# Two small sums and minima of a softmax written as reductions over two neighbouring columns

## The chip, the cores and the metric

The kernel runs on one core of a Trainium2 chip. The metric is device time of one execution in microseconds (us); lower is better. The engines named below work beside each other, each through its own queue in order: TensorE (PE, with its weight loads as PEld), VectorE (DVE), ScalarE (ACT), GpSimd (POOL) and SyncE (SP, which here issues transfers). SBUF is the on-chip working memory, PSUM the memory that TensorE writes to.

## What is computed

The program is one step of a two-layer trunk over 256 context tokens and 1024 latent tokens of width 1024, in float32. The change lies in the first layer's grouped-query attention of the latent tokens (8 query heads, 2 key heads, 1024 latent keys and 256 cached context keys in one softmax):

```
keys = jnp.concatenate([axial_rope(k), ctx_k.astype(k.dtype)], axis=1)
values = jnp.concatenate([vals, ctx_v.astype(vals.dtype)], axis=1)
b_out = blocked_attention(axial_rope(q), keys, values)
...
def one_block(qblk):
    s = jnp.einsum('bqngd,bsnd->bngqs', qblk, k).astype(jnp.float32) * scale
    p = jax.nn.softmax(s, axis=-1).astype(v.dtype)
    return jnp.einsum('bngqs,bsnd->bqngd', p, v)
```

The softmax needs one maximum and one denominator for each row of 1280 scores.

## The kernel before

The whole program is written for one core with the order of every engine's instructions fixed by hand: in the attention, each job has a table of events at fractional slots, and `run_jobs` emits the events of up to four jobs that overlap, sorted by slot. So a row of an engine's queue is where the table puts it, and an engine does its queue in that order.

In the latent attention a job is one pair of 128-query tiles (a = 0 and 1) of one head; there are 32 such jobs (4 pairs of tiles, 8 heads), then two jobs of another class for the context tokens. The 1280 scores of a tile come in two parts: 1024 latent scores in a PSUM tile of class A (`scores`, L704 and L705) and 256 cached ones in PSUM tile C (`cached_scores`, L711 and L712). For each part there is a negated maximum (`maxima`, L719 and L717) and, from the exponential's accumulator, a part of the denominator (`exp`, L730). So each tile has two maxima in neighbouring columns of a small SBUF tile `sm` and two partial denominators in two other neighbouring columns. `bias` (L723) takes the smaller of the two negated maxima. `scale` adds the two denominators (L734), takes the reciprocal (L735), and then lets POOL multiply the 1280 probabilities by it in two instructions of 640 columns (L737). All of `bias`, L734 and L735 are DVE instructions on 128 x 1 elements.

After that the scaled probabilities are transposed by TensorE into a PSUM tile B (`turn`, L374, four 128 x 128 blocks at a time), split into a high part by ACT (`hi`, L384) and a low part by DVE (`lo`, L390), and multiplied with the values (`values`, L408). `store` (L355 on ACT, L356 on DVE) ends a job. In every eighth job the queries of the next pair of tiles are also loaded and split, by ACT (L637) and POOL (L638); such a job is called a query-loading job below.

In one period of the steady stage, DVE's order is: lo 4 of an older job, lo 0, maxima 0, lo 1, the cached maxima, store, bias 0, lo 2, scale 1, lo 3, maxima 1, scale 0, bias 1. So of a job's two L734, that of tile 0 stands ahead of a bias and two L390, and that of tile 1 between two L390.

Of the kernel before, what the change touches and what calls it, by code (L numbers as in the profile page):

```python
# [15 lines left out]
ALU = mybir.AluOpType  # L16
AX = mybir.AxisListType
# [32 lines left out]
def trunk_kernel(ctx: ExitStack, tc: tile.TileContext, A: dict, O: dict):  # L50
    nc = tc.nc
    PE, ACT, DVE, POOL, SP = nc.tensor, nc.scalar, nc.vector, nc.gpsimd, nc.sync
# [147 lines left out]
    def rstd_of(ss, n, scale, eps=EPS):  # L200

        v, r = sm(n), sm(n)
        DVE.tensor_scalar(v, ss, scale, eps, op0=ALU.mult, op1=ALU.add)
        POOL.tensor_tensor(r, v, mhalf[:, 0:n], op=ALU.pow)  # L204
        return r
# [444 lines left out]
    def gate_steps(l, w):  # L650

        for j in range(2):
            c = slice(512 * j, 512 * j + 512)
            total = [t2([P, 512]) for _ in range(2)]
            for k in range(KT):
                r = raw([P, 512])
                SP.dma_start(r, A["mod_w"][l, rows(k), (3 * w + 2) * D + 512 * j : (3 * w + 2) * D + 512 * j + 512])
                yield
                for c in range(2):
                    if k == 0:  # L660
                        DVE.tensor_scalar(total[c], r, cond[:, k, c : c + 1], None, op0=ALU.mult)
                    else:
                        DVE.scalar_tensor_tensor(total[c], r, cond[:, k, c : c + 1], total[c], op0=ALU.mult, op1=ALU.add)
            bias, acc = raw([32, 512]), bank((32, 512))
            SP.dma_start(bias, A["mod_b"][l, 3 * w + 2, 32 * j : 32 * j + 32])
            for c in range(2):
                PE.matmul(acc, pick[:, c, :], total[c], start=c == 0, stop=c == 1)
            yield
            DVE.tensor_tensor(bias, acc, bias, op=ALU.add)
            SP.dma_start(gate_d[l, w, :, 512 * j : 512 * j + 512], bias[0:2])  # L670
# [16 lines left out]
    class Latent(Job):  # L687
# [32 lines left out]

        def bias(self, a):
            m = self.sm[:, 2 * a : 2 * a + 2]
            DVE.tensor_tensor(self.sm[:, 8 + a : 9 + a], m[:, 0:1], m[:, 1:2], op=ALU.min)  # L723

        def exp(self, a, c):
            if self.p[a] is None:
# [4 lines left out]

        def scale(self, a):
            z, p = self.sm[:, 10 + a : 11 + a], self.p[a]
            DVE.tensor_tensor(z, self.sm[:, 4 + 2 * a : 5 + 2 * a], self.sm[:, 5 + 2 * a : 6 + 2 * a], op=ALU.add)  # L734
            DVE.reciprocal(z, z)  # L735
            for c in (slice(0, 640), slice(640, 1280)):
                POOL.tensor_tensor(p[:, c], p[:, c], z.to_broadcast([P, 640]), op=ALU.mult)  # L737
# [967 lines left out]
```

## Time and profile before

| what | value |
|---|---|
| median of 3 runs | 3441.93 us (3436.46 to 3443.43) |
| the profiled execution | 3447.16 us |
| its span, first to last instruction | 3445.4 us |
| granted TensorE clock, mean | 0.982 of full speed |
| busy: PE | 3265.6 us (95%) |
| busy: DVE | 2094.1 us (61%) |
| busy: ACT | 1266.3 us (37%) |
| busy: POOL | 1179.4 us (34%) |

The busy times are sums over the whole span; the latent attention is only its part from about 205 to 466 us. All durations quoted further on come from the profiled execution, which lies 5.2 us (0.15%) above the median of the runs and has 1.8 us outside its span.

### The profile page before, as it was taken

To read this page: it belongs to the slowest core of one execution; us is meant where nothing else is said; L and a number is where in the kernel's file an instruction comes from. 1 tells how busy PE (TensorE), PEld (TensorE's weight loads), DVE (VectorE), ACT (ScalarE), POOL (GpSimd) and SP (SyncE) were. 2 spreads that over 40 slices of the span, in tenths; PEclk is the share of its full clock that TensorE was granted. 3 is DMA by queue.
4 is the path that set the end of the run, shared out by engine and by line. 5 is a ranking of instruction groups with operands and counts; after the bars stand their busy time and mean duration, and the time that the engine had idled before them with its cause. 6 is when DMAs were issued, how large, how long until landed. Compare 5 with 4: busy or idle time off the path is not lost. (4 is left out here: it accounts for less than half of the span.)

```text
span 3445.4 us, 44445 instructions
## 1 busy us (share of the span) xinstructions
PE 3265.6 (95%) x17258; PEld 2723.2 (79%) x17258; DVE 2094.1 (61%) x3589; ACT 1266.3 (37%) x2529; POOL 1179.4 (34%) x742
## 2 busy tenths in 40 slices
PE   5789999999999999999899999999999999999998
PEld 3667777888878878888778888887778888888886
DVE  7879988546666664344866666666574444344347
ACT  3467863451111111112566666656531111111113
POOL 3556667451111111113644433335221111111134
PEclk8889999999999999999999999999999999999999
DMA  5210023442222221112411111113431111111124
GB/s 208 69 37 14 19 89 114 155 145 87 87 87 88 88 84 40 38 37 86 177 58 45 47 47 45 49 65 97 126 116 45 39 42 43 37 37 37 38 91 165
DMA packets 106211, 260.03 MB, mean 75 GB/s; under 512 B 10240, under 2 KB 45952, under 8 KB 106000
## 3 DMA queue, kind: packets, MB, share of 16 engines
q1 hardware_dynamic: 106000, 257.20, 22.5%
q8 instruction: 135, 2.21, 0.3%
q14 instruction: 76, 0.62, 0.1%
HBM read 221.34 MB, written 35.82 MB: 75 GB/s over the span
## 5 line engine op out<-in xcount | busy, mean ns | idle before, releaser
L1097 DVE TENSOR_TENSOR s<-s,B 128x512 f32<-128x512 f32 x840 | 559.9, 685 | 565.2 <-PE B L192 564.5
L176 POOL TENSOR_TENSOR w<-raw,w 128x1024 fp32r<-128x1024 f32 x163 | 402.6, 2472 | 1408.0 <-ACT w L175 1403.8
L190 PE MATMUL A<-hh,w 128*128 128x512 f32 (+1 forms) x2112 | 755.0, 357 | 3.5 <-DVE s L330 2.2
L192 PE MATMUL A<-hh,w 128*128 128x512 f32 (+1 forms) x2112 | 750.3, 355 | 2.8 <-POOL w L176 2.8
L191 PE MATMUL A<-hl,w 128*128 128x512 f32 (+1 forms) x2112 | 747.7, 354 | 0.0
L190 PEld LDWEIGHTS A<-hh,w 128*128 128x128 f32 x2112 | 397.5, 188 | 69.5 <-issue 5.9
L192 PEld LDWEIGHTS A<-hh,w 128*128 128x128 f32 x2112 | 397.2, 188 | 66.0 <-POOL w L176 4.0
L191 PEld LDWEIGHTS A<-hl,w 128*128 128x128 f32 x2112 | 397.4, 188 | 62.8
L175 ACT CAST w<-raw 128x1024 fp32r<-128x1024 f32 x166 | 174.2, 1049 | 712.7 <-PE B L191 416.1
L190 PE MATMUL B<-w,s 128*128 128x512 f32 x880 | 351.2, 399 | 14.2 <-DVE s L1097 13.5
L192 PE MATMUL B<-w,s 128*128 128x512 f32 x880 | 348.2, 396 | 9.7 <-DVE s L176 8.7
L191 PE MATMUL B<-w,s 128*128 128x512 f32 x880 | 344.0, 391 | 0.0
L1078 ACT ACTIVATE t<-A,c 128x512 f32<-128x512 f32 (+1 forms) x132 | 81.2, 615 | 703.2 <-PE A L192 703.2
L374 PE MATMUL B<-c,s 128*128 128x128 f32 x1344 | 205.8, 279 | 46.8 <-DVE w L390 23.4
L374 PEld LDWEIGHTS B<-c,s 128*128 128x128 f32 x1344 | 155.8, 141 | 90.6 <-DVE w L390 35.7
L190 PE MATMUL C<-hh,w 128*128 128x512 f32 (+1 forms) x576 | 213.0, 370 | 5.2 <-ACT s L1200 1.8
L390 DVE TENSOR_TENSOR t<-B,t 128x512 fp32r<-128x512 f32 (+2 forms) x216 | 127.6, 591 | 142.9 <-ACT t L384 129.6
L190 PEld LDWEIGHTS B<-w,s 128*128 128x128 f32 x880 | 165.3, 188 | 59.2 <-DVE s L1097 27.0
L1079 DVE TENSOR_TENSOR t<-t,A 128x512 f32<-128x512 f32 (+1 forms) x132 | 78.9, 598 | 218.6 <-ACT t L1078 218.6
L192 PEld LDWEIGHTS B<-w,s 128*128 128x128 f32 x880 | 165.4, 188 | 52.5 <-DVE s L176 12.7
L192 PE MATMUL C<-hh,w 128*128 128x512 f32 (+1 forms) x576 | 205.4, 357 | 0.0
L191 PE MATMUL C<-hl,w 128*128 128x512 f32 (+1 forms) x576 | 205.3, 356 | 0.0
(283 smaller groups left out, 6178.9 us busy)
## 6 DMA issues: line engine op xcount, KB each, us to landing
raw<-wall SPq DMA_DIRECT2D x171, 512.0 KB, 3.3
raw<-mod_w SPq DMA_DIRECT2D x72, 512.0 KB, 3.9
x_d<-s SPq DMA_DIRECT2D x30, 512.0 KB, 2.6
w<-wall SPq DMA_DIRECT2D x22, 512.0 KB
raw<-x SPq DMA_DIRECT2D x20, 512.0 KB, 3.9
s<-x_d SPq DMA_DIRECT2D x20, 512.0 KB
s<-wall SPq DMA_DIRECT2D x17, 512.0 KB, 3.4
w<-mod_w SPq DMA_DIRECT2D x16, 512.0 KB, 9.3
```

Of the source, the lines that this page charges most:

```text
L175: ACT.copy(hi, src)
L176: (eng or DVE).tensor_tensor(lo, src, f32(hi), op=ALU.subtract)
L190: PE.matmul(out, sh, mh, start=i == 0, stop=False)
L191: PE.matmul(out, sh, ml, start=False, stop=False)
L192: PE.matmul(out, sl, mh, start=False, stop=i == n - 1)
L374: PE.transpose(tr[:, at : at + P], self.p[a][:, col : col + P], ident)
L390: DVE.tensor_tensor(tl[:, 0:n], tr[:, 0:n], f32(th[:, 0:n]), op=ALU.subtract)
L1078: ACT.activation(s, acc[:, 0, 0:n], AF.Silu, bias=zerob)
L1079: DVE.tensor_tensor(s, s, acc[:, 1, 0:n], op=ALU.mult)
L1097: DVE.tensor_tensor(yt, yt, part, op=ALU.add)
```

## The change

`bias` and the addition in `scale` each used an instruction with two one-column inputs, `tensor_tensor`. They now use `tensor_reduce` over one input of two neighbouring columns, with the same operation (minimum, addition) and the same one-column output.

```
@@ -720,7 +720,7 @@
         def bias(self, a):
             m = self.sm[:, 2 * a : 2 * a + 2]
-            DVE.tensor_tensor(self.sm[:, 8 + a : 9 + a], m[:, 0:1], m[:, 1:2], op=ALU.min)
+            DVE.tensor_reduce(self.sm[:, 8 + a : 9 + a], m, axis=AX.X, op=ALU.min)
@@ -731,7 +731,7 @@
         def scale(self, a):
             z, p = self.sm[:, 10 + a : 11 + a], self.p[a]
-            DVE.tensor_tensor(z, self.sm[:, 4 + 2 * a : 5 + 2 * a], self.sm[:, 5 + 2 * a : 6 + 2 * a], op=ALU.add)
+            DVE.tensor_reduce(z, self.sm[:, 4 + 2 * a : 6 + 2 * a], axis=AX.X, op=ALU.add)
             DVE.reciprocal(z, z)
             for c in (slice(0, 640), slice(640, 1280)):
                 POOL.tensor_tensor(p[:, c], p[:, c], z.to_broadcast([P, 640]), op=ALU.mult)
```

It concerns 128 DVE instructions: 64 of L723 and 64 of L734, two of each in every latent job. No instruction is added, removed or moved: every engine's queue has the same rows in the same order, and each of the 128 waits for the same engine as before.

## Rows read from the trace of the kernel before

**Rows 1.** Busy time of each engine in two stretches: the attention, what follows it.
```profile
core 0: us, PE busy (x) PEld busy (x) DVE busy (x) ACT busy (x) POOL busy (x), PEclk, DMA share, GB/s
...
215.00:466.00 251.00, 225.19 (x1559) 192.47 (x1558) 240.92 (x453) 199.63 (x437) 169.61 (x138) 0.99 0.07 22
...
483.00:560.00 77.00, 75.78 (x355) 59.69 (x354) 68.55 (x105) 32.50 (x55) 51.03 (x31) 1.00 0.34 108
```
**Rows 2.** Groups by line and form, 200 to 480 us: busy us, mean ns | idle before.
```profile
L734 DVE TENSOR_TENSOR sm<-sm 128x1 f32<-128x1 f32 x64 | 34.5, 538 | 1.3 <-ACT s L730 1.3
...
L723 DVE TENSOR_TENSOR sm<-sm 128x1 f32<-128x1 f32 x64 | 15.8, 247 | 0.5
```
**Rows 3.** One line's instructions: minimum, median and maximum duration in ns.
```profile
L734 DVE TENSOR_TENSOR sm<-sm x64: 142/152/1019, 209.5 to 470.4; 128x1 f32<-128x1 f32 x64
...
L723 DVE TENSOR_TENSOR sm<-sm x64: 137/142/1223, 207.4 to 465.5; 128x1 f32<-128x1 f32 x64
```
**Rows 4.** DVE in order of time, one ordinary job: start us, duration us, instruction.
```profile
329.58 0.15 DVE L734 TENSOR_TENSOR sm<-sm 128x1 f32<-128x1 f32 x1
329.77 0.17 DVE L735 RECIPROCAL sm<-sm 128x1 f32<-128x1 f32 x1
...
331.57 1.02 DVE L734 TENSOR_TENSOR sm<-sm 128x1 f32<-128x1 f32 x1
332.62 0.16 DVE L735 RECIPROCAL sm<-sm 128x1 f32<-128x1 f32 x1
...
332.76 1.28 DVE L390 TENSOR_TENSOR w<-B,w 128x512 fp32r<-128x512 f32 x2
```
**Rows 5.** POOL, ACT and PE in the same job, in order of time.
```profile
330.10 2.47 POOL L737 TENSOR_TENSOR s<-s,sm 128x640 f32<-128x640 f32 x2 [2.68 <-DVE sm L735]
...
331.25 0.71 PE L374 MATMUL B<-c,s 128*128 128x128 f32 x4
...
331.99 0.59 ACT L384 CAST w<-B 128x512 fp32r<-128x512 f32 x1 [0.53 <-PE B L374]
...
332.49 0.40 PE L705 MATMUL A<-s,w 128*128 128x512 f32 x1
333.50 0.66 PE L374 MATMUL B<-c,s 128*128 128x128 f32 x4 [0.61 <-DVE w L390]
```
**Rows 6.** A query-loading job in order of time: DVE, ACT, POOL.
```profile
295.23 0.68 DVE L723 TENSOR_TENSOR sm<-sm 128x1 f32<-128x1 f32 x1
...
298.68 1.07 ACT L384 CAST w<-B 128x512 fp32r<-128x512 f32 x2
...
298.82 0.60 DVE L734 TENSOR_TENSOR sm<-sm 128x1 f32<-128x1 f32 x1 [0.33 <-ACT s L730]
...
299.48 2.60 POOL L638 TENSOR_TENSOR w<-raw,w 64x512 fp32r<-64x512 f32 x2
...
299.53 1.22 DVE L723 TENSOR_TENSOR sm<-sm 128x1 f32<-128x1 f32 x1
300.68 1.27 DVE L390 TENSOR_TENSOR w<-B,w 128x512 fp32r<-128x512 f32 x2
```
**Rows 7.** POOL and DVE in an earlier stage, in order of time.
```profile
69.11 2.35 POOL L176 TENSOR_TENSOR s<-raw,s 128x256 fp32r<-128x256 f32 x4 [2.03 <-ACT s L175]
...
70.36 0.69 DVE L479 TENSOR_REDUCE sm<-s 128x8 f32<-128x512 f32 x1 [0.36 <-ACT s L478]
71.08 0.40 DVE L203 TENSOR_SCALAR sm<-sm 128x8 f32<-128x8 f32 x1
```
**Rows 8.** POOL and DVE in the second layer's attention, in order of time.
```profile
1782.24 2.62 POOL L1273 TENSOR_TENSOR w<-s,w 64x1024 fp32r<-64x1024 f32 x1
...
1782.55 0.15 DVE L1421 RECIPROCAL sm<-sm 128x1 f32<-128x1 f32 x1
```
**Rows 9.** One line's instructions for other reductions: minimum, median and maximum ns.
```profile
L479 DVE TENSOR_REDUCE sm<-t x10: 276/285/289, 62.4 to 188.8; 128x2 f32<-128x128 f32 x10
L479 DVE TENSOR_REDUCE sm<-s x8: 677/679/687, 70.4 to 172.7; 128x8 f32<-128x512 f32 x8
...
L1409 DVE TENSOR_REDUCE sm<-A x128: 406/414/425, 1762.1 to 2404.9; 128x1 f32<-128x256 f32 x128
```

More of the change, by code (lines that the diff above doesn't have):

```diff
@@ L722, in bias @@
             m = self.sm[:, 2 * a : 2 * a + 2]
-            DVE.tensor_tensor(self.sm[:, 8 + a : 9 + a], m[:, 0:1], m[:, 1:2], op=ALU.min)
+            DVE.tensor_reduce(self.sm[:, 8 + a : 9 + a], m, axis=AX.X, op=ALU.min)
         def exp(self, a, c):
@@ L733, in scale @@
             z, p = self.sm[:, 10 + a : 11 + a], self.p[a]
-            DVE.tensor_tensor(z, self.sm[:, 4 + 2 * a : 5 + 2 * a], self.sm[:, 5 + 2 * a : 6 + 2 * a], op=ALU.add)
+            DVE.tensor_reduce(z, self.sm[:, 4 + 2 * a : 6 + 2 * a], axis=AX.X, op=ALU.add)
             DVE.reciprocal(z, z)
```

## The prediction

> **What bounds the kernel now.** I read the whole-kernel busy shares first, and they mislead here: PE is busy 95% of the span and DVE 61%, so a change on DVE looks free. The change touches only the latent attention, so the view that counts is the table of busy time by stretch [rows 1]. In the 251.0 us from 215 to 466 us, DVE is busy 240.92 us (96%), PE 225.19 us (90%), ACT 199.63 us (80%) and POOL 169.61 us (68%). In this stretch DVE is the fullest engine, and PE has some 26 us of gaps. After it, from 483 to 560 us, PE is busy 75.78 of 77.0 us (98%).
>
> Next, the groups by line for this stretch [rows 2]. The two lines of the diff do the same kind of work, one addition or minimum of one column, and should cost the same. L723 has a mean of 247 ns, L734 of 538 ns. The spread says more [rows 3]: both have a median near 0.15 us (142 and 152 ns) but maxima of 1223 and 1019 ns. So some instances stand still. The time order shows where [rows 4, 5]: the L734 at 329.58 takes 0.15 us with POOL idle; the one at 331.57 takes 1.02 us and ends at 332.59. POOL's two L737 run from 330.10 to 332.57. The addition, whose two inputs both lie in SBUF, is held until POOL's instruction ends. In the query-loading job the same happens to L723: it starts at 299.53, just after POOL's L638 at 299.48 (two in 2.60 us, so the first ends near 300.78), and ends at 300.75 [rows 6].
>
> Held time in all: 34.5 − 64 × 0.152 = 24.8 us for L734 and 15.8 − 64 × 0.142 = 6.7 us for L723, together 31.5 us [rows 2, 3]. Reading all 128 in order of time, I count 27 L734 of 0.95 to 1.02 us, one in each ordinary job but the first, and in each of the 4 query-loading jobs one L734 near 0.60 and two L723 near 0.67 and 1.22 us. As a check: 27 × 0.86 + 4 × 0.45 = 25.0 us for L734.
>
> **The change, part by part.**
> First, is a reduction held as well? The trace has one instance with an SBUF input beside a running POOL instruction [rows 7]: POOL's four L176 fill 69.11 to 71.46, and L479, a reduction of 128x512 from SBUF, starts at 70.36 and takes 0.69 us, its unhindered 679 ns [rows 9]. Right after it a TENSOR_SCALAR of 128x8 at 71.08 takes 0.40 us, until 71.48, when POOL is done. So in one and the same stretch the reduction passes and another form is held. I take it that L723 and L734 are no longer held.
>
> Second, the reduction's own price. No row has two columns. The reductions give 285 ns for 128 columns and 679 ns for 512 [rows 9], so (679 − 285) / 384 = 1.03 ns a column and, from 285 − 126 × 1.03, an estimated 155 ns for two. Bounds: no cheaper than the 137 ns minimum of L723 [rows 3], since nothing this short is cheaper; no dearer than 285 ns, the smallest SBUF reduction. I take 155, the straight line's value: 3 ns more on L734 and 13 ns more on L723, 64 × 0.016 = 1.0 us in all. The upper bound would cost 64 × (0.133 + 0.143) = 17.7 us if all of it lay on the path, the lower bound gives back 1.3 us.
> The Trainium skill speaks against the change in "VectorE: DVE Perf Modes", section "Rules for kernel authors": `tensor_reduce` runs at the base rate, is "the slowest DVE op" and is to be avoided on a hot path. The rows above put 1.03 ns on each column and a start of some 0.15 us, so by them the rule costs nothing at two columns; by the rule taken as a general penalty, at the 285 ns bound, the gain summed below would be 25.1 + 1.0 − 17.7 = 8.4 us.
>
> Third, an ordinary job. Without the hold, L735 follows the L734 of 331.57 by 0.19 us (as 329.77 does 329.58) and the first L390 follows L735 by 0.14 us (332.62 to 332.76) [rows 4]: it starts at 331.90 instead of 332.76, 0.86 us earlier. The second L390 of the pair would start 0.60 us later (1.28 for both, 0.68 for one), at 332.50. But it needs ACT's L384 of 331.99, which ends at 332.58 [rows 5]. That one waits for TensorE's transposes of 331.25 to 331.96, half of which read what POOL has scaled by 330.10 + 1.24 = 331.34; this chain starts from the unhindered L734 at 329.58 and doesn't get shorter. So the second L390 starts at 332.60 instead of 332.76 + 0.60 = 333.36: 0.76 us earlier, not 0.86. DVE's queue is full from there to the next 329.58-like L734, so all that follows moves with it. For TensorE: its transposes at 333.50 waited for the first L390 [rows 5], 0.61 us after the end of L705 at 332.89. L390 now ends at 331.90 + 0.68 = 332.58, and TensorE, whose score matmuls follow each other by 0.23 us, is ready at 332.72: a gain of 0.78 us. Both give 0.76 to 0.78 us; I take 0.76. 27 × 0.76 = 20.5 us.
>
> Fourth, a query-loading job [rows 6]. The L723 held at 295.23 saves nothing: the next L734, at 298.82, waits for ACT's exponential, and ACT is full there. Behind it, L734 loses 0.45 us and L723 1.08 us. The first L390 would start at 298.82 + 0.19 + 0.14 = 299.15 (with the ordinary job's spacings), needs the first of ACT's two L384 (298.68 + 0.59 = 299.27), and the second L390 needs the other (299.75) and 0.60 us after the first: 299.89 instead of 301.28. That is 1.39 us; 4 × 1.39 = 5.6 us.
>
> Sum: 20.5 + 5.6 − 1.0 = 25.1 us, of 31.5 us held. What comes after the attention is TensorE's [rows 1], with transfers at a 0.34 share, so the gain is kept. The profiled execution becomes 3447.2 − 25.1 = 3422.1 us, the median of the runs, 5.2 us lower, 3441.9 − 25.1 = 3416.8 us.
>
> **The rivals.**
> *The hold moves one instruction on.* The reciprocal L735 follows L734 and never ran beside POOL in this stretch before. If it is held, L734 to L390 takes as long as now. Against it: a reciprocal of the same shape ran 0.15 us at 1782.55 inside a POOL instruction [rows 8]. The same end is reached if a two-column reduction is held after all; one row [rows 7], of another shape, speaks against it. What would be left is at most the L723 part, 4 × 1.08 = 4.3 us: 3438 to 3442 us. Chance 0.09.
> *The gain is cut by another wait.* With DVE earlier, the ring over POOL, TensorE and ACT closes the period, and I followed it only at one job's places; ACT, 80% busy, orders its exponentials between the L384. If half the gain is lost: 3425 to 3435 us. Chance 0.14.
> *More than forecast.* If the L723 of 295.23 counts too and the ring gives way to the full 0.86 us, the gain is the held 31.5 us and some of TensorE's gaps: 3407 to 3411 us. Chance 0.05.
> *Slower.* A reduction costs DVE more than the hold does. Its place is DVE's queue, four of them a job; it decides from 0.76 / 4 = 0.19 us extra each, a reduction of 0.34 us. The next row above that, a one-column result at 414 ns [rows 9], would cost 4 × 0.26 − 0.76 = 0.28 us a job, 32 × 0.28 = 9 us: 3451 us. That row has 256 columns out of PSUM, and the line through the others leaves no room for it. Chance 0.03.
>
> **How the numbers follow.** The forecast has 0.69, with its own range 3411 to 3423 us. With the larger gain, and the nearer half of the cut one, the range 3407 to 3428 us holds about 8 in 10. About 0.2% (7 us) is what a measurement of this kernel can tell from no change: faster 0.88 (forecast, cut, larger), same 0.09, slower 0.03.
>
> **What the profile after would show.** L723 and L734 as TENSOR_REDUCE with minimum, median and maximum all near 0.15 us; their sum 64 × 0.31 = 19.8 us instead of 50.3; L735 unchanged at 0.16 us although POOL now runs beside it; POOL's second pair of L737 joined to the first; TensorE's wait for L390 ahead of its transposes gone; ordinary jobs about 7.3 us apart. I am wrong if L735 or the reductions show a tail, if the period shrinks by less than 0.5 us, or if a later stage gives it back.

## The result and the profile after

The changed kernel takes 3416.76 us (median of 4 runs, 3413.36 to 3417.94) against 3440.4 us of the kernel before (4 runs): a ratio of 0.993, 95% interval 0.9913 to 0.9948. Run again later beside three of the experiments, it took 3421.2 us against 3446.6 us, 0.9919 (0.9904 to 0.9935). The forecast was 3416.8 us.

The first rows to compare are those of the two lines, as in [rows 3]; with them the reciprocal that follows and POOL's scaling. Columns: count, minimum/median/maximum ns, first and last start.

```profile
L723 DVE TENSOR_REDUCE sm<-sm x64: 134/136/157, 206.0 to 437.1; 128x1 f32<-128x2 f32 x64
...
L734 DVE TENSOR_REDUCE sm<-sm x64: 143/145/157, 208.1 to 441.9; 128x1 f32<-128x2 f32 x64
...
L735 DVE RECIPROCAL sm<-sm x64: 163/164/167, 208.3 to 442.1; 128x1 f32<-128x1 f32 x64
...
L737 POOL TENSOR_TENSOR s<-s,sm x128: 1248/1253/1258, 208.6 to 443.7; 128x640 f32<-128x640 f32 x128
```

The tails of 1223 and 1019 ns are gone. In the kernel before, 39 of the 128 instructions (31 L734, 8 L723) started while POOL ran an instruction, and every one of them ended 0.01 to 0.02 us after that instruction's end; the other 89 started with POOL idle and took at most 164 ns. Now 74 of the 128 start beside a running POOL instruction, and none takes more than 157 ns. POOL's instructions take what they took (a median of 1256 ns before), so nothing was handed to it, and the reciprocal, which now runs beside POOL, was not held.

The same place in an ordinary job, in order of time (start us, duration us), which answers to [rows 4, 5]: DVE first, then POOL, ACT and PE.

```profile
315.55 0.14 DVE L734 TENSOR_REDUCE sm<-sm 128x1 f32<-128x2 f32 x1
...
317.52 0.15 DVE L734 TENSOR_REDUCE sm<-sm 128x1 f32<-128x2 f32 x1
317.70 0.17 DVE L735 RECIPROCAL sm<-sm 128x1 f32<-128x1 f32 x1
317.78 0.14 DVE L723 TENSOR_REDUCE sm<-sm 128x1 f32<-128x2 f32 x1
317.83 1.43 DVE L390 TENSOR_TENSOR w<-B,w 128x512 fp32r<-128x512 f32 x2
```
```profile
316.06 4.89 POOL L737 TENSOR_TENSOR s<-s,sm 128x640 f32<-128x640 f32 x4 [2.28 <-PE B L374]
```
```profile
317.95 0.59 ACT L384 CAST w<-B 128x512 fp32r<-128x512 f32 x1 [0.52 <-PE B L374]
```
```profile
318.45 0.40 PE L705 MATMUL A<-s,w 128*128 128x512 f32 x1
318.69 0.60 PE L374 MATMUL B<-c,s 128*128 128x128 f32 x4
```

POOL now works from 316.06 to 320.95 without a break, and the three small DVE instructions L734, L735 and L723 pass it at full speed. The pair of L390 starts 0.31 us after L734 and not 1.19. It takes 1.43 us where it took 1.28: the second waits for ACT's L384, which ends at 318.54, as the forecast's third step said. TensorE's transposes follow its score matmuls at 0.24 us, without the 0.61 us wait of [rows 5].

The busy time of the stretch, the row that answers to the first of [rows 1]:

```profile
core 0: us, PE busy (x) PEld busy (x) DVE busy (x) ACT busy (x) POOL busy (x), PEclk, DMA share, GB/s
215.00:442.00 227.00, 223.23 (x1583) 194.64 (x1580) 213.64 (x455) 198.48 (x443) 169.22 (x138) 1.00 0.09 28
```

PE is now busy 98% of the stretch and DVE 94%, where it was 90% and 96%. From the first maximum (L719) to the start of the last L734 the attention takes 441.93 − 203.90 = 238.03 us against 470.36 − 205.31 = 265.05 us: 27.0 us less. After it the program takes 2973.0 us against 2975.0 us: the gain is kept.

Not all of the 27.0 us belongs to the change. In the opening jobs TensorE's granted clock rises from 0.50 (the 1.2 GHz level) to 1.00 (2.4 GHz). In the kernel before it rises 12.6 us after the first maximum. In this profile of the changed kernel it rises 8.6 us after it, in the second profile of the same kernel (the change once more, below) 12.7 us after it. The rows show 4 us of each, from 8 to 12 us after the first maximum: before, after, and the change once more (columns as in the view above). The attention of the second profile takes 239.5 us, and nearly all of the difference between the two, 1.37 us, lies in one opening job, whose work falls into this stretch. So with the clock rising at the same place as before, the change gives 265.0 − 239.5 = 25.6 us, and the other 1.4 us came with the earlier clock. What set the moment of the rise was not tried.

```profile
213.30:217.30 4.00, 3.26 (x11) 2.15 (x10) 3.00 (x5) 2.57 (x7) 3.51 (x3) 0.50 0.00 0
...
211.90:215.90 4.00, 3.26 (x21) 2.41 (x20) 2.88 (x6) 3.14 (x9) 3.89 (x4) 0.93 0.00 0
...
214.40:218.40 4.00, 3.27 (x11) 2.17 (x10) 2.19 (x5) 2.54 (x7) 3.86 (x4) 0.50 0.00 0
```

### The profile page after: what moved, and what is told of

It is laid out like the page before. It is cut to its first block, busy times and chain, and to the rows that moved or that the text cites. A ratio compares the mean times of both kernels' runs of the same rounds, so it can differ in the third digit from the quotient of the medians.

```text
span 3414.9 us, 44445 instructions
## 1 busy us (share of the span) xinstructions
PE 3260.3 (95%) x17258; PEld 2720.6 (80%) x17258; DVE 2062.5 (60%) x3589; ACT 1262.0 (37%) x2529; POOL 1178.4 (35%) x742
## 5 line engine op out<-in xcount | busy, mean ns | idle before, releaser
L374 PE MATMUL B<-c,s 128*128 128x128 f32 x1344 | 206.9, 278 | 25.9 <-DVE raw L356 14.3
L390 DVE TENSOR_TENSOR t<-B,t 128x512 fp32r<-128x512 f32 (+2 forms) x216 | 127.6, 591 | 143.0 <-ACT t L384 129.7
L192 PEld LDWEIGHTS B<-w,s 128*128 128x128 f32 x880 | 165.5, 188 | 54.6 <-DVE s L176 14.8
```

The costliest lines, as they stand in the source:

```text
L192: PE.matmul(out, sl, mh, start=False, stop=i == n - 1)
L374: PE.transpose(tr[:, at : at + P], self.p[a][:, col : col + P], ident)
L390: DVE.tensor_tensor(tl[:, 0:n], tr[:, 0:n], f32(th[:, 0:n]), op=ALU.subtract)
```

## The experiments

The theory is that a DVE instruction with two inputs out of SBUF cannot start while POOL runs an instruction, and waits for that one's end; and that after the change the period of a job is closed by a ring over DVE, POOL, TensorE and ACT. The first four experiments below ran on one chip beside 18 runs of the kernel before (median 3446.0 us), the other four on another chip beside 9 (3446.6 us). "Ordinary job" is the mean spacing of L734 over six jobs of the trace; the last column is the busy time of all 128 instructions.

| kernel | median us | ratio to before (95%) | ordinary job us | L723 + L734, sum us |
|---|---|---|---|---|
| before | 3446.0 | 1 | 8.03 | 50.3 |
| only the sum reduced | 3437.6 | 0.9972 (0.9961 to 0.9983) | 7.77 | 40.4 |
| only the minimum reduced | 3439.6 | 0.9977 (0.9968 to 0.9986) | 8.02 | 42.3 |
| both with a scalar operand | 3427.5 | 0.9946 (0.9934 to 0.9958) | 7.39 | 25.9 |
| minimum reduced, POOL in quarters | 3427.6 | 0.9947 (0.9935 to 0.996) | 7.58 | 32.2 |
| the change again | 3421.2 | 0.9919 (0.9904 to 0.9935) | 7.25 | 18.4 |
| change, more work on the ring | 3426.1 | 0.994 (0.9927 to 0.9952) | 7.32 | 18.4 |
| change, the same work beside it | 3421.3 | 0.9926 (0.9913 to 0.9938) | 7.30 | 18.4 |
| change, POOL 256 + 1024 | 3418.1 | 0.9916 (0.9903 to 0.993) | 7.19 | 18.4 |

**Only the sum.**
```
 def bias(self, a):
     DVE.tensor_tensor(self.sm[:, 8 + a : 9 + a], m[:, 0:1], m[:, 1:2], op=ALU.min)
...
 def scale(self, a):
-    DVE.tensor_tensor(z, self.sm[:, 4 + 2 * a : 5 + 2 * a], self.sm[:, 5 + 2 * a : 6 + 2 * a], op=ALU.add)
+    DVE.tensor_reduce(z, self.sm[:, 4 + 2 * a : 6 + 2 * a], axis=AX.X, op=ALU.add)
```


> The denominators' sum (L734) is a reduction, the minimum (L723) stays a two-input instruction. Theory A, a two-input DVE instruction is held by whatever POOL instruction it meets: the L723 behind L734 and L735 now meets POOL's second L737 and is held there, about 0.7 us in every ordinary job, so most of the gain is lost: 3431 to 3437 us, with L723 maxima still about 1 us and many more of them. Theory B, the parts add, L734 carries 24.8 of the 31.5 us held: 3440 - 19 = 3421 us.

Measured 8.4 us less than before, not 19. DVE in order of time, and POOL's instruction in the same job:
```profile
335.76 4.90 POOL L737 TENSOR_TENSOR s<-s,sm 128x640 f32<-128x640 f32 x4 [2.92 <-DVE sm L735]
...
337.23 0.14 DVE L734 TENSOR_REDUCE sm<-sm 128x1 f32<-128x2 f32 x1
337.41 0.16 DVE L735 RECIPROCAL sm<-sm 128x1 f32<-128x1 f32 x1
337.49 0.76 DVE L723 TENSOR_TENSOR sm<-sm 128x1 f32<-128x1 f32 x1
338.17 1.27 DVE L390 TENSOR_TENSOR w<-B,w 128x512 fp32r<-128x512 f32 x2
```
L734 and the reciprocal pass, and the two-input L723 two places on is held until 338.25, when the second of POOL's four instructions ends (335.76 + 2 × 1.24 = 338.24). The hold has moved, not gone. It is shorter only because DVE arrives later by then. L723 is held like this in 26 ordinary jobs and takes 0.73 to 0.76 us in each, where before it was held in none of them. In all 35 of the 64 are held, against 8 before:
```profile
L723 DVE TENSOR_TENSOR sm<-sm x64: 140/515/1117, 208.9 to 458.0; 128x1 f32<-128x1 f32 x64
```

**Only the minimum.**
```
 def bias(self, a):
-    DVE.tensor_tensor(self.sm[:, 8 + a : 9 + a], m[:, 0:1], m[:, 1:2], op=ALU.min)
+    DVE.tensor_reduce(self.sm[:, 8 + a : 9 + a], m, axis=AX.X, op=ALU.min)
```


> The minimum (L723) is a reduction, the sum (L734) stays a two-input instruction. Theory A: L734 is held as before in the ordinary jobs, only the four L723 of the query-loading jobs are freed: 4 x 1.08 = 4 us less, 3436 us. Together with the other half alone this is far less than the 24 us of both. Theory B, the parts add: 3440 - 5 = 3435 us; the two theories differ here only in the sum.

6.4 us less; the ratio's interval of 0.9968 to 0.9986 is 4.8 to 11.0 us, so somewhat more than the 4 us expected. In the trace, eight jobs take 65.0 us instead of 66.4, so each freed query-loading job gives 1.4 us and not 1.08. Ordinary jobs stay at 8.02 us and L734 nearly as it was, 33.3 us in all against 34.5:
```profile
L734 DVE TENSOR_TENSOR sm<-sm x64: 148/172/1022, 211.8 to 467.0; 128x1 f32<-128x1 f32 x64
```
The halves alone give 8.4 and 6.4 us, together 14.8, the whole 25.4 on the same kind of count. So the parts don't add. With the sum reduced, the minimum takes over its hold; the other way round no hold moves, the sum merely keeps its own.

**A scalar operand in place of the second input.**
```
-    DVE.tensor_tensor(self.sm[:, 8 + a : 9 + a], m[:, 0:1], m[:, 1:2], op=ALU.min)
+    DVE.tensor_scalar(self.sm[:, 8 + a : 9 + a], m[:, 0:1], m[:, 1:2], None, op0=ALU.min)
...
-    DVE.tensor_tensor(z, self.sm[:, 4 + 2 * a : 5 + 2 * a], self.sm[:, 5 + 2 * a : 6 + 2 * a], op=ALU.add)
+    DVE.tensor_scalar(z, self.sm[:, 4 + 2 * a : 5 + 2 * a], self.sm[:, 5 + 2 * a : 6 + 2 * a], None, op0=ALU.add)
```


> Both lines as tensor_scalar: one column as the tensor input, the other as the per-partition scalar operand. Theory A, the hold comes from the second tensor input read out of SBUF: no hold, all 128 near 0.15 us, 3417 us as with the change. Rival, only a reduction passes POOL and any form that reads two separate SBUF columns is held: 3440 us as before.

```profile
L723 DVE TENSOR_SCALAR sm<-sm x64: 193/196/216, 206.2 to 440.9; 128x1 f32<-128x1 f32 x64
...
L734 DVE TENSOR_SCALAR sm<-sm x64: 202/204/215, 208.3 to 445.9; 128x1 f32<-128x1 f32 x64
```
No tail: the same two SBUF columns, read as an input and a scalar operand, are not held. For one-column operands it is the second tensor input that makes DVE wait, and a reduction is only one way round it. This doesn't hold for every `tensor_scalar`: the one of 128x8 at 71.08 in [rows 7] has one tensor input and was held, and so it is after the change (391 ns, where the others of its form take 171 to 172). What sets that form apart was not tried. The time, 18.4 us less, is short of the 3417 us expected on two counts: the kernel before, too, took 5.6 us more here than beside the change, and the form costs 196 and 204 ns where the reduction costs 136 and 145. With some 0.06 us more on each of four instructions, ordinary jobs are 0.13 us longer than with the change (7.39 against 7.25).

**Shorter POOL instructions**, with the sum still a two-input instruction and the minimum reduced:
```
-    for c in (slice(0, 640), slice(640, 1280)):
-        POOL.tensor_tensor(p[:, c], p[:, c], z.to_broadcast([P, 640]), op=ALU.mult)
+    for c in (slice(i, i + 320) for i in range(0, 1280, 320)):
+        POOL.tensor_tensor(p[:, c], p[:, c], z.to_broadcast([P, 320]), op=ALU.mult)
```


> The minimum is a reduction, the sum stays a two-input instruction, and POOL scales in four instructions of 320 columns instead of two of 640. Theory A, a hold lasts until the running POOL instruction ends: an L734 is held for at most one piece, 0.3 to 0.6 us instead of 1.0, and ordinary jobs become about 0.4 us shorter, 3425 to 3430 us. Rival, DVE waits until POOL has nothing left to do: L734 is held 1.0 to 1.2 us as before, 3436 to 3442 us.

```profile
326.65 5.47 POOL L737 TENSOR_TENSOR s<-s,sm 128x320 f32<-128x320 f32 x8 [2.19 <-DVE sm L735]
...
328.12 0.63 DVE L734 TENSOR_TENSOR sm<-sm 128x1 f32<-128x1 f32 x1
328.78 0.16 DVE L735 RECIPROCAL sm<-sm 128x1 f32<-128x1 f32 x1
```
POOL has eight instructions back to back from 326.65 to 332.12, 0.68 us apart; L734 is held until 328.75, by when the third ends (326.65 + 3 × 0.69 = 328.72), and runs before POOL is done. So a hold lasts to the end of the running POOL instruction, not of POOL's queue. Ordinary jobs are 0.44 us shorter than with the minimum alone reduced, the time 12 us less. The hold itself became 0.39 us shorter (1.02 to 0.63); shorter pieces also release TensorE's transposes earlier, and what that gives here was not separated. Against the kernel before the time is 18.4 us less, more than the 10 to 15 us expected.

**The change once more**, for the three that follow.

> The changed kernel once more, on the chip of the three runs beside it. 0.993 of the kernel before, ordinary jobs 7.25 us apart on average.

As expected: 0.9919, with the expected 0.993 in its interval, and 7.25 us.

**More DVE work on and beside the ring.** One line behind the minimum, for tile 0 in one kernel and for tile 1 in the other; the results are read by nothing, so the output stays that of the change:
```
     DVE.tensor_reduce(self.sm[:, 8 + a : 9 + a], m, axis=AX.X, op=ALU.min)
+    [DVE.tensor_reduce(spare[:, i : i + 1], m, axis=AX.X, op=ALU.min) for i in range(2) if a == 0]
```


> The change, with two more reductions that nothing reads behind the minimum of tile 0 (L723), each worth some 0.06 to 0.08 us of DVE's queue. Theory A, the period is now closed by a ring DVE - POOL - TensorE - ACT - DVE that passes this place: jobs 0.12 to 0.16 us longer, 4 to 5 us in all against the change. Rival, TensorE's own work closes it: DVE has 13 us of slack in the stretch and nothing is seen, under 1 us.

> The same two reductions behind the minimum of tile 1, where the ring doesn't pass and DVE then waits about 0.2 us for ACT between its two L390. Theory A: at most 0.03 us a job, 0 to 1 us against the change. Rival, DVE's whole queue closes the period: as long as with the other place, 4 to 5 us.

DVE behind tile 0's minimum in the first kernel, and behind tile 1's in the second:
```profile
324.81 0.15 DVE L723 TENSOR_REDUCE sm<-sm 128x1 f32<-128x2 f32 x1
324.88 0.21 DVE L724 TENSOR_REDUCE spare<-sm 128x1 f32<-128x2 f32 x2
325.12 0.69 DVE L390 TENSOR_TENSOR w<-B,w 128x512 fp32r<-128x512 f32 x1
```
```profile
324.72 0.14 DVE L723 TENSOR_REDUCE sm<-sm 128x1 f32<-128x2 f32 x1
324.77 0.21 DVE L724 TENSOR_REDUCE spare<-sm 128x1 f32<-128x2 f32 x2
324.89 1.36 DVE L390 TENSOR_TENSOR w<-B,w 128x512 fp32r<-128x512 f32 x2
```
The two reductions push the next L390 back by some 0.12 us in either place. By the medians the first costs 4.9 us against the change and the second nothing, which is what theory A said, but the intervals of the three overlap, and the spacing of the jobs is finer and tells more. With the change, jobs are alternately about 7.15 and 7.36 us long. On the ring, the long ones become 7.45 to 7.50 and the short ones stay (7.14 to 7.17); beside it, the short ones become 7.24 and the long ones stay (7.33 to 7.38). So both places are near critical, each in one half of the jobs, at +0.07 and +0.04 us on the average, where theory A said 0.12 to 0.16 and at most 0.03. Neither theory is right alone. What this would mean is that the ring closes only every second job, and that the others are closed by a path through the place behind tile 1's minimum, probably over the first L390 to TensorE's transposes; which path closes which job is argued, not shown. 31 jobs at +0.07 us are 2 us, so the 4.9 us by the medians are more than the trace bears out.

**An earlier first piece from POOL**, on top of the change:
```
-    for c in (slice(0, 640), slice(640, 1280)):
-        POOL.tensor_tensor(p[:, c], p[:, c], z.to_broadcast([P, 640]), op=ALU.mult)
+    for c in (slice(0, 256), slice(256, 1280)):
+        POOL.tensor_tensor(p[:, c], p[:, c], z.to_broadcast([P, c.stop - c.start]), op=ALU.mult)
```


> The change, with POOL's two scalings of 256 and 1024 columns instead of 640 and 640, so that TensorE's first transposes, which read the first 256, are released about 0.63 us earlier. Theory A, the ring closes the period: it shrinks until TensorE's own work, about 7.1 us a job, closes it; 0.1 us x 31, 3 to 4 us faster than the change. Rival, TensorE or DVE closes it already: no difference, within 1 us.

```profile
L737 POOL TENSOR_TENSOR s<-s,sm x128: 610/1254/1897, 210.4 to 443.0; 128x256 f32<-128x256 f32 x64, 128x1024 f32<-128x1024 f32 x64
```
The first piece takes 0.61 us instead of 1.25. Jobs become 7.11 and 7.23 to 7.30 us long, 7.19 on the average against 7.25; 27 ordinary jobs at 0.06 us are 1.6 us. The whole attention takes 236.2 us, 3.3 us less than with the change beside it (239.5), but only 1.8 us less than in the first profile of the change (238.0): here, too, the granted clock rose early, 9.3 us after the first maximum against 12.7. By the medians it is 3.2 us faster (3418.1 against 3421.2), but the intervals lie on each other (0.9903 to 0.993 and 0.9904 to 0.9935): a small gain that the spacing of the jobs shows and the timing can't confirm. The jobs gave way by about half of what theory A said, 0.06 and not 0.1 us, which would fit a ring that closes only every second job.

## Why the prediction was right

- **What bounds.** DVE was the fullest engine of the stretch, and taking 31.5 us of held time from it shortened the attention by 27.0 us, 25.6 of them without the earlier clock. The whole-kernel shares (PE 95%, DVE 61%) would have said that nothing can be won there.
- **The hold.** Shown by three kernels: with the minimum left as it was, it is held in the sum's place; with a scalar operand the hold goes without a reduction; with shorter POOL instructions it gets shorter. The Trainium skill, "SBUF — State Buffer", section "Who interferes with whom", says that VectorE's second tensor input comes through a read interface that it shares with GpSimd, so that an instruction with two SBUF inputs contends with a GpSimd instruction that reads SBUF and whichever issues second is blocked, and that `tensor_reduce` never contends on trn2. All these runs agree as far as DVE waits for POOL: 39 of 39 two-input instructions that started beside POOL before were held, and none of 74 reductions after. Whether POOL also waits for DVE, no run here shows.
- **The reduction's price.** The step that was mis-sized: 155 ns were taken, 136 and 145 measured (18.4 us for all 128, against 18.8 for as many unheld instructions before: 64 × 0.152 + 64 × 0.142). The 1.0 us that it was charged wasn't there. The Trainium skill's rule that a reduction is the slowest DVE operation ("VectorE: DVE Perf Modes", section "Rules for kernel authors") doesn't hold at two columns: it was the cheapest of the three forms tried (136 and 145 ns, against 142 and 152 unheld with two inputs, 196 and 204 with a scalar operand).
- **An ordinary job.** 0.76 us were forecast; 8.025 − 7.253 = 0.77 us measured. That is an average. The gain alternates from job to job between 0.84 us, nearly the whole 0.86 us of the hold, and 0.69 to 0.74 us. So the cut from 0.86 to 0.76 us, which the forecast worked out at one place for all jobs, stands only as a mean, and that it fits so closely is in part luck. That two paths would end at nearly the same place (0.76 and 0.78) fits both places being near critical; that each of them closes half of the jobs is argued, not shown.
- **A query-loading job.** Eight jobs took 66.38 us and take 59.62, 6.76 us less; less 7 × 0.772 that leaves 1.36 us, forecast 1.39. The minimum alone already makes eight jobs 1.4 us shorter, so the size is right, but the share of 0.45 us that the forecast gave to L734 in it is not confirmed.
- **The sum.** 27 × 0.77 + 4 × 1.36 = 26.2 us, against 27.0 us in the first profile and 25.6 us in the second. In the second, the held L734 of one opening job (214.97 us in the trace before) gives nothing while the clock is at 0.50, and 26 × 0.77 + 4 × 1.36 = 25.5 us comes close to what was measured. Forecast: 25.1, with the price that wasn't there and with that job counted.
- **The rivals.** The reciprocal is not held (at most 167 ns beside POOL). The gain was not cut. TensorE's wait for L390 ahead of its transposes, which the forecast said would be gone, is not wholly gone: of 23.2 us on PE 2.6 us in 7 waits are left, and of 35.7 us on its weight loads 12.3 us. With PE busy 223.23 of 227.00 us, little of the latter can cost time.

The waits, before from 200 to 480 us, then after from 200 to 456 us (waiting engine, line, releaser: us in total, times, longest):
```profile
PEld B L374 <- DVE w L390: 35.7, 30, 2.1
PE B L374 <- DVE w L390: 23.2, 31, 1.7
...
PEld B L374 <- DVE w L390: 12.3, 51, 0.9
...
PE B L374 <- DVE w L390: 2.6, 7, 0.5
```

The match of the median, 3416.76 us against a forecast of 3416.8, is luck in its closeness. The medians of the result lie 23.6 us apart (3440.4 and 3416.76) and those of the later pair 25.4 us, with intervals of several us. The kernel before gave 3440.4 us beside the change and 3446.0 and 3446.6 us later. The profiled executions of before and after lie 30.4 us apart, of which only 27.0 us fall into the attention.

## What to carry to other kernels

A short instruction whose maximum is seven times its median may be waiting inside its own busy time, as here, so look at the spread of each group before its mean, and at what the other engines did when it ended. Where VectorE and GpSimd work side by side, try to give the small VectorE operations one tensor input: a reduction over two neighbouring columns, or one column with a scalar operand, were not held here. Change all of the queue's neighbours together, since a hold that is removed from one instruction can fall on the next two-input one, as it did from the sum to the minimum: the halves of this change gave 8 and 6 us, the whole 25.

## What was not expected of the hardware

- `tensor_scalar` with a 128 x 1 scalar operand out of SBUF takes 196 to 204 ns, 50 to 60 ns more than an unheld two-input instruction or a two-column reduction on the same columns; the jobs were 0.13 us longer with it.
- A held DVE instruction gets in between two POOL instructions that stand back to back, so the length of one POOL instruction, not of POOL's queue, bounds the price: 0.63 us in an ordinary job with 320 columns, where it was 1.02 with 640.
- Jobs alternate between two lengths, 0.2 us apart (7.15 and 7.36 us). In the long ones L356 starts 0.71 us after L717 and the next L723 0.46 us after L356; in the short ones it is 0.60 and 0.33 us. The kernel shows one difference between them: `store` writes heads of even number to partitions 0 to 63 and heads of odd number to 64 to 127 (`base = 64 * ((h + i) % 2)`), and the L356 of every long job is that of an odd head. No run tried it, so the cause stays open.
